# Fixed places for weight splits, and matmuls moved into the waits of two recurrences

## The chip, the cores and the metric

The program runs on one core of a Trainium2 chip. The metric is the device time in microseconds (us) of one execution. Five engines work side by side, each through its own list of instructions in order: TensorE (PE, matmuls and the weight loads before them), VectorE (DVE), ScalarE (ACT), GpSimd (POOL) and SyncE (SP, which only issues DMAs here). They wait for each other by semaphores.

## What is computed

One layer of a decoder for 512 prompt tokens and 8 samples of 4 tokens (544 columns in all): a SwiGLU feed-forward block, then time mixing (RWKV-7) beside a short gated convolution, then a second feed-forward block, with a layer norm after each. The part around the change is the time mixing. For each head of 64 the state S goes through all tokens:

```
S <- S diag(w) + (S (-kk)) (kk*a)^T + v k^T ;  o = S r
o = group_norm(o) ;  o = o + (sum r*k*r_k) v ;  y = o * g
mix = concat(y, y_conv) @ w_out
```

`g` is the gate, a low-rank product of its own (`sigmoid(gd) @ g_lora_up`), which does not depend on S. The prompt starts from S = 0, each sample from a stored S.

## The kernel before

All matrices lie transposed: features on the 128 partitions, tokens along the free dimension, in two halves (`HALF`: 256 and 288 columns). Matrix products of full precision are made of three matmuls: every weight tile is loaded in fp32 (`raw`), copied by ACT into a rounded high part (line 135 of `wsplit`), and DVE subtracts to get the low part (line 136). High times high, high times low and low times high add up in PSUM (`mm3`, lines 152 to 154). Such a tile of 1024 columns is called a weight, and its two operations a **split**. Two `raw` buffers and three or four split buffers (`hl`) turn over.

The 512 prompt tokens are cut into 8 chunks of 64. The heads go in two groups (g = 0, 1) of two tiles of two heads. For a group the kernel first builds the chunks' triangular matrices (`scores`, `elim`, `rounds`), and then goes through the chunks in order (`chain`, called from `recur`). This is the **recurrence**, and one chunk is a **step**, 0 to 7. A step is a chain over the engines: PE makes a product with the state (line 1230); ACT copies it to `W` (1233); PE multiplies by the inverse `XT` (1239); DVE copies one half of U (1240) and ACT the other (1241); PE multiplies by `BK` (1248); DVE adds this to S and scales it (1256, 1258), which makes the S of the next step. The output of the step before is made on the side (`out_u`, 1209; `out_s`, 1215; copy to `O` in 1217).

While the step's last DVE operations run, PE works on **fillers**: generators in the queue `bg` that yield their expected time; `slots` puts one step and then some 1500 ns of fillers in turn (18 matmuls). In the first recurrence the fillers are the convolution's products (`conv`, `conv_mm`: three weights for each of the tiles i = 0, 1, 2), in the second the output projection (`wout0`, then `wout1`, with weights `wo_c` and `wo_0`, and `last0` with `wo_1`). Inside a step PE has nothing else to do but small work that `small(c, k)` starts at three places of step c: k = 0 between 1230 and 1239, k = 1 between 1239 and 1248, k = 2 after the state update. That small work is

- `sample`: the samples' part of the recurrence. It loads the stored states (1285), makes two blocks of 32 small matmuls with them (1293), copies the results (1299 to 1303), makes a step like the prompt's (1308, 1315, 1324), and then for each of two tiles a product with its masked U (1333) and two DVE operations on the states (1335, 1336), and stores them (1338). The table `when` says at which (c, k) it goes on.
- `gnorm(g, 0, ...)`: the group norm of the first half of the columns: a product that centres (1349), a square (1350), the mean (1354), Ln and Exp (1355, 1357), the gate's product (1362), and three DVE operations with gain, bias and gate (1365 to 1367). Its first two parts run in step 5, the last after step 7. `gnorm(g, 1, ...)` does the second half after the recurrence.

PSUM has eight buffers: three named `mm` (from `big`), five named `sm` (from `sm`). Waits between engines and the buffers' turns are worked out when the program is built, from what reads and writes what. The order on each engine is worked out then too: a planner goes through expected durations and issues, on each engine, what is ready, the instruction traced first by the program going first. `after(x, y)` and `issue_after(y)` add an order (x not ahead of y on that engine) and no wait on the chip. In `slots`, what the fillers after step c trace may not stand ahead of the U copy and the state update of step c - 1. What is traced after the recurrence, outside of `slots`, has no such bound.

Of the kernel before, what the change touches and what calls it, by code (L numbers as in the profile page):

```python
# [14 lines left out]
AF = mybir.ActivationFunctionType  # L15
# [4 lines left out]
P = 128  # L20
# [41 lines left out]
def body(ctx: ExitStack, tc: tile.TileContext, xT, gu1, wd1, win, wo_c, wo_0, wo_1, gu2, wd2, wl, ln3, eye, lora, vec, cst,  # L62
# [30 lines left out]
    def sm():  # L93
        return ps.tile([P, 512], F32, name="sm", bufs=5)
# [39 lines left out]
    def wsplit(hl, raw, a, b):  # L134
        seen["hi"] = ACT.activation(hl[:, 0, a:b], raw[:, a:b], AF.Copy)  # L135
        seen["lo"] = DVE.tensor_tensor(hl[:, 1, a:b], raw[:, a:b], hl[:, 0, a:b].bitcast(F32), op=OP.subtract)  # L136
        return seen["lo"]

    def split(hi, lo, x):
# [16 lines left out]
                yield 6 * ((c1 - c0) / 2.4 + 3)  # L156

    bg = deque()
    seen = dict(rs=None, hhl=None, pe=None, fill=None, uv=None, new=[], old=[])

    def crit(e):
        seen["pe"] = e
# [1029 lines left out]
    def v2(q, rows=slice(0, P)):  # L1192
        return q[rows, :128].rearrange("p (d t) -> p d t", d=2)

    def chain(g, cp, small):


        tl = cp.tile
        AR = ARs[g]
        heads = [(pl, par) for pl in range(2) for par in range(2)]  # L1200
        Ss, q2, uv = {}, None, []

        def at(q, pl, par):
            return q[R(par), pl * 64:pl * 64 + 64]

        def out_u(c):
            q = sm()
            for pl, par in heads:
                crit(PE.matmul(at(q, pl, par), UV[:, pl, par, c, :], SC[:, pl, par, c, 64:128], start=(pl == 0 or c == 0),
                               stop=(c == 0), skip_group_check=True))  # L1210
            return q

        def out_s(c, q):
# [3 lines left out]
            o = ACT.activation(O[:, :, c, :], v2(q), AF.Copy)  # L1217
            for e in uv:
                after(o, e)

        for c in range(8):
            if c < 7:
                Sn = Ss[c + 1] = tl([P, 2, 2, 64], F32, name="S", bufs=3)
                with tc.issue_after(seen["pool"].ins):
                    for par in range(2):
                        POOL.tensor_copy(Sn[R(1 - par), :, par, :], UV[R(1 - par), :, par, c + 1, :])
            q = sm()
            for pl, par in heads:
                k = slice(0, P) if c else R(1 - par)
                crit(PE.matmul(at(q, pl, par), SC[k, pl, par, c, 0:64], Ss[c][:, pl, par, :] if c else UV[k, pl, par, c, :],  # L1230
                               start=True, stop=True))
            W = tl([P, 2, 64], F32, name="W", bufs=2)
            ACT.activation(W, v2(q), AF.Copy)
            if c:
                q2 = out_u(c - 1)
            small(c, 0)
            qs = (sm(), sm())
            for pl, par in heads:
                crit(PE.matmul(at(qs[par], pl, par), XT[R(par), c, pl, :], W[R(par), pl, :], start=True, stop=True))
            seen["uv"] = DVE.tensor_copy(UV[R(0), :, 0, c, :], v2(qs[0], R(0)))  # L1240
            seen["new"] = [ACT.copy(UV[R(1), :, 1, c, :], v2(qs[1], R(1)))]
            uv[:] = seen["new"]
            if c:
                out_s(c - 1, q2)
            small(c, 1)
            q = sm()
            for par, pl in heads:
                crit(PE.matmul(at(q, pl, par), BK[:, pl, par, c, :], UV[:, pl, par, c, :], start=True, stop=True))
            pe = Pe[:, 2 * g:2 * g + 2, c:c + 1].to_broadcast([P, 2, 64])
            if c == 7:  # L1250
                SF = tl([P, 2, 64], F32, name="W", bufs=2)
            for par in range(2):
                dst = Sn[R(par), :, par, :] if c < 7 else SF[R(par)]
                src = v2(q, R(par))
                if c:
                    DVE.tensor_tensor(dst, Ss[c][R(par), :, par, :], src, op=OP.add)
                    src = dst
                upd = DVE.tensor_tensor(dst, src, pe[R(par)], op=OP.mult)
            seen["new"].append(upd)
            small(c, 2)  # L1260
            if c == 7:
                dma(wkvp_o[:, 2 * g:2 * g + 2, :], SF)
                out_s(7, out_u(7))
            yield 1

    def recur(g, cp, run):
        sam, gn = sample(g, cp), gnorm(g, 0, cp)
        when = {(2, 0): 1, (2, 1): 1, (2, 2): 1, (3, 0): 1, (3, 1): 1, (4, 2): 1, (5, 2): 2, (6, 2): 2}

        def small(c, k):  # L1270
            for _ in range(when.get((c, k), 0)):
                next(sam, None)
            if c == 5 and k < 2:
                next(gn, None)

        slots(chain(g, cp, small), run)
        for x in (sam, gn):
            for _ in x:
                pass

    def sample(g, cp):
# [3 lines left out]
        dma(S0, s0[:, 2 * g:2 * g + 2])  # L1285
        WT = tl([P, 2, 32], F32, name="WT")
        SI = tl([P, 2, 2, 64], F32, name="SI")
        q = sm()
        qv = q[:, :256].rearrange("p (d x t) -> p d x t", d=2, x=2)
        for pl in range(2):  # L1290
            for b in range(NSEQ):
# [45 lines left out]
            yield 500  # L1337
        dma(wkvs_o[:, 2 * g:2 * g + 2], S0)

    def gnorm(g, h, cp):  # L1340
        t0, t1, _ = SEG[h]
        n = (256, 288)[h]
        t1 = t0 + n
# [10 lines left out]
            PE.matmul(q[:, :n], bo, sq[pl][:, :n], start=True, stop=True)  # L1354
            ACT.activation(sq[pl][:, :n], q[:, :n], AF.Ln, scale=1.0 / 64, bias=epsg)
        for pl in range(2):
            ACT.activation(sq[pl][:, :n], sq[pl][:, :n], AF.Exp, scale=-0.5)
        yield 600
        for pl in range(2):
            p = 2 * g + pl  # L1360
            qs.append(sm())
            PE.matmul(qs[pl][:, :n], lo[:, 1, P * p:P * p + P], sgd[:, t0:t1], start=True, stop=True)
        for pl in range(2):
            p, y = 2 * g + pl, sq[pl]
            DVE.scalar_tensor_tensor(y[:, :n], xc[pl][:, :n], col(V_GNG, p), sq[pl][:, :n], op0=OP.mult, op1=OP.mult)
            DVE.scalar_tensor_tensor(y[:, :n], y[:, :n], col(V_GNB, p), bvs[g][pl][:, t0:t1], op0=OP.add, op1=OP.add)
            DVE.tensor_tensor(o[pl], y[:, :n], qs[pl][:, :n], op=OP.mult)
            if g == 0:
                dma(ycd[:, p, t0:t1], o[pl])
            else:  # L1370
                split(xhl[:, 0, p, t0:t1], xhl[:, 1, p, t0:t1], o[pl])
# [18 lines left out]
    def conv(i):  # L1390
        u = tl([P, 2 + TP + 6 * NSEQ], F32, name="cu")
        cc = tl([P, T], F32, name="cc")
        zc = tl([P, T], F32, name="zc")
        us = u[:, 514:].rearrange("p (b t) -> p b t", t=6)
        POOL.memset(u[:, 0:2], 0.0)
        POOL.tensor_copy(us[:, :, 0:2], cst_[:, i])
        for h in range(2):
            yield from conv_mm(14 + 3 * i, h, partial(conv_c, cc))
        for h in range(2):
            yield from conv_mm(15 + 3 * i, h, partial(conv_u, cc, u, us))  # L1400
        taps = conv_taps(i, u, us, zc)
        next(taps)
        for h in range(2):
            for n, x in enumerate(conv_mm(16 + 3 * i, h, partial(conv_z, zc))):
                if n in (0, 2):
                    next(taps, None)
                yield x
            for _ in taps:
                pass
        dma(ycd[:, 4 + i], zc)  # L1410

    def conv_mm(i, h, use):
        c0, c1 = HALF[h]
        w = wget(i)
        q = big()
        yield from mm3(q[:, :c1 - c0], w, xhl, range(KD), c0, c1)
        use(q, h, c0, c1)
        yield 300
# [73 lines left out]
    cst0 = ExitStack()  # L1492
    cp = pool(cst0, "chain0")
    slots(rounds(0), 600)
    recur(0, cp, 1500)
    weave("g0", gnorm(0, 1, cp))
    cst0.close()
    ast.close()
    w4 = pool(ast, "w4")
    wstate["ex_hl"] = [lambda: w4.tile([P, 2, 1024], F32R, name="hl", bufs=1)]  # L1500
    weave("s2", pairs[2].scores())
    bg.appendleft(own_b(3))
    need(3, 2)
    take(FILL["p3"])
# [42 lines left out]
            for k, y in ys + [(7, zc)]:  # L1547
                ysplit(k, y, c0, c1)

    w1s, fin = {}, []  # L1550

    def add_z(d, h, o, n=1):
        c0, c1 = HALF[h]
# [3 lines left out]
    def wout0():  # L1557
# [41 lines left out]
    def wout1():  # L1599
# [66 lines left out]
    ast.close()  # L1666
    mst.close()
    yst.close()

    f2.s1[0] = s1  # L1670
    f2.open()
# [97 lines left out]
```

## Time and profile before

| | us |
|---|---|
| three timed runs | 1072.36, 1072.5, 1072.72 |
| median | 1072.5 |
| the profiled execution | 1072.43 |
| its span, first to last instruction | 1070.7 |
| PE busy | 1050.7 |
| DVE / ACT / POOL busy | 844.7 / 583.2 / 154.9 |
| first recurrence, steps 0 to 7 | from 503.9 to 544.1 |
| second recurrence, steps 0 to 7 | from 617.5 to 658.3 |

The recurrences' times are from PE's timeline: the first matmul of line 1230 in step 0, and the first filler after step 7's output. The mean clock granted to PE was 0.998 of full speed. A time like 504.76 is us from the span's start; "L1239" is line 1239 of the kernel before; "idle before" in brackets is how long an engine stood still ahead of an instruction, and which instruction of another engine ended that. A matmul's end is modelled and overlaps the next, so what an instruction costs PE is read from one start to the next.

### The profile page before, as it was taken

To read this page: it belongs to the slowest core of one execution; us is meant where nothing else is said; L and a number is where in the kernel's file an instruction comes from. 1 tells how busy PE (TensorE), PEld (TensorE's weight loads), DVE (VectorE), ACT (ScalarE), POOL (GpSimd) and SP (SyncE) were. 2 spreads that over 40 slices of the span, in tenths; PEclk is the share of its full clock that TensorE was granted. 3 is DMA by queue.
4 is the path that set the end of the run, shared out by engine and by line. 5 is a ranking of instruction groups with operands and counts; after the bars stand their busy time and mean duration, and the time that the engine had idled before them with its cause. 6 is when DMAs were issued, how large, how long until landed. Compare 5 with 4: busy or idle time off the path is not lost.

```text
span 1070.7 us, 22612 instructions
## 1 busy us (share of the span) xinstructions
PE 1050.7 (98%) x9178; PEld 1010.5 (94%) x9178; DVE 844.7 (79%) x1557; ACT 583.2 (54%) x1070; POOL 154.9 (14%) x273
## 2 busy tenths in 40 slices
PE   9999999999999999999999999999999999999997
PEld 8999999999999999899889988999999999999996
DVE  6797888979875777793578657988979888797757
ACT  5746555555553668654444435767555555555524
POOL 0111121211200022133101200001211212121000
PEclk9999999999999999999999999999999999999999
DMA  8558585676854233324145724434766848668512
GB/s 292 132 112 186 120 199 135 145 172 132 186 118 158 79 88 109 85 82 99 41 143 161 173 81 139 141 119 79 152 165 137 200 101 194 143 137 189 147 43 84
DMA packets 91528, 144.48 MB, mean 135 GB/s; under 512 B 34848, under 2 KB 52384, under 8 KB 91296
## 3 DMA queue, kind: packets, MB, share of 16 engines
q1 hardware_dynamic: 68144, 110.76, 34.2%
q0 software_dynamic: 22848, 31.72, 19.2%
q8 instruction: 72, 1.18, 0.4%
q10 hardware_dynamic: 432, 0.56, 0.2%
q14 instruction: 32, 0.26, 0.1%
HBM read 128.81 MB, written 9.75 MB: 129 GB/s over the span
## 4 chain that ended last, share of the span: by engine, by line
PE 76%; DVE 13%; ACT 7%; issue 2%; DMA 2%; POOL 0%; ACTq 0%; DVEq 0%; SPq 0%
PE mm L553 9%; PE mm L554 9%; PE mm L555 9%; PE sm L553 6%; PE sm L554 6%; PE sm L555 6%; PE mm L152 6%; PE mm L153 5%; PE mm L154 5%; DVE hhl L141 2%; ACT hl L135 2%; DVE hl L136 2%; PE sm L441 1%; PE sm L1166 1%; PE mm L784 1%
## 5 line engine op out<-in xcount | busy, mean ns | idle before, releaser
L136 DVE TENSOR_TENSOR hl<-raw,hl 128x1024 fp32r<-128x1024 f32 (+3 forms) x230 | 270.2, 1179 | 63.7 <-ACT hl L135 62.6
L135 ACT ACTIVATE hl<-raw 128x1024 fp32r<-128x1024 f32 (+3 forms) x230 | 232.9, 1020 | 69.7 <-DVE raw L519 43.5
L152 PE MATMUL mm<-xhl,hl 128*128 128x256 f32 (+1 forms) x704 | 209.2, 299 | 0.5 <-ACT xhl L140 0.5
L153 PE MATMUL mm<-xhl,hl 128*128 128x256 f32 (+1 forms) x704 | 203.0, 289 | 0.4 <-DVE xhl L141 0.4
L154 PE MATMUL mm<-xhl,hl 128*128 128x256 f32 (+1 forms) x704 | 202.0, 287 | 0.0
L152 PEld LDWEIGHTS mm<-xhl,hl 128*128 128x128 f32 x704 | 132.0, 188 | 6.9 <-issue 2.0
L153 PEld LDWEIGHTS mm<-xhl,hl 128*128 128x128 f32 x704 | 132.3, 188 | 2.7 <-issue 1.0
L154 PEld LDWEIGHTS mm<-xhl,hl 128*128 128x128 f32 x704 | 132.3, 188 | 0.3 <-issue 0.2
L555 PE MATMUL sm<-xhl,hl 128*128 128x272 f32 x432 | 125.2, 290 | 0.0
L554 PE MATMUL sm<-xhl,hl 128*128 128x272 f32 x432 | 124.4, 288 | 0.0
L553 PE MATMUL sm<-xhl,hl 128*128 128x272 f32 x432 | 124.1, 287 | 0.0
L553 PE MATMUL mm<-tv,hl 128*128 128x272 f32 x288 | 83.3, 289 | 0.3
L555 PE MATMUL mm<-tv,hl 128*128 128x272 f32 x288 | 83.4, 290 | 0.0
L554 PE MATMUL mm<-tv,hl 128*128 128x272 f32 x288 | 83.1, 288 | 0.0
L553 PEld LDWEIGHTS sm<-xhl,hl 128*128 128x128 f32 x432 | 81.4, 188 | 0.0
L554 PEld LDWEIGHTS sm<-xhl,hl 128*128 128x128 f32 x432 | 81.3, 188 | 0.0
L555 PEld LDWEIGHTS sm<-xhl,hl 128*128 128x128 f32 x432 | 81.2, 188 | 0.0
L532 POOL DMA_DIRECT2D raw<-in_wd x32 | 39.2, 1462 | 288.0 <-DVE hlb L141 225.2
L526 POOL DMA_DIRECT2D raw<-in_gu x36 | 43.3, 1203 | 203.5 <-DVE hlb L141 143.8
L553 PE MATMUL mm<-hhl,hl 128*128 128x272 f32 x192 | 56.4, 300 | 0.3
L554 PE MATMUL mm<-hhl,hl 128*128 128x272 f32 x192 | 55.9, 291 | 0.8 <-DVE hhl L141 0.2
L553 PEld LDWEIGHTS mm<-tv,hl 128*128 128x128 f32 x288 | 54.2, 188 | 1.9 <-ACT cpb L620 1.9
(416 smaller groups left out, 2716.0 us busy)
## 6 DMA issues: line engine op xcount, KB each, us to landing
raw<-in_gu SPq DMA_DIRECT2D x84, 512.0 KB, 4.5
raw<-in_gu POOLq DMA_DIRECT2D x36, 512.0 KB, 6.6
raw<-in_wd SPq DMA_DIRECT2D x32, 512.0 KB, 4.5
raw<-in_win SPq DMA_DIRECT2D x26, 512.0 KB, 3.6
raw<-in_wd POOLq DMA_DIRECT2D x32, 256.0 KB, 6.0
z<-sv POOLq DMA_DIRECT2D x16, 272.0 KB, 8.4
raw<-in_wo_c SPq DMA_DIRECT2D x8, 512.0 KB, 3.6
raw<-in_wd SPq DMA_DIRECT2D x8, 384.0 KB, 3.2
```

The source lines that it names most:

```text
L135: seen["hi"] = ACT.activation(hl[:, 0, a:b], raw[:, a:b], AF.Copy)
L136: seen["lo"] = DVE.tensor_tensor(hl[:, 1, a:b], raw[:, a:b], hl[:, 0, a:b].bitcast(F32), op=OP.subtract)
L141: return DVE.tensor_tensor(lo, x, hi.bitcast(F32), op=OP.subtract)
L152: PE.matmul(out, wh, src[:, 0, k, c0:c1], start=(start and i == 0), stop=False)
L153: PE.matmul(out, wh, src[:, 1, k, c0:c1], start=False, stop=False)
L154: seen["fill"] = PE.matmul(out, wl, src[:, 0, k, c0:c1], start=False, stop=(stop and i == n - 1))
L441: PE.matmul(o[i][h][:, :c1 - c0], block(hl, v, k), xhl[:, y, k, c0:c1], start=(k == 0 and j == 0), stop=(k == KD - 1 and j == 2), skip_gro ...
L526: POOL.dma_start(x.rearrange("p (s c) -> p s c", s=2), bass.AP(tensor=a11.tensor, offset=a11.offset, ap=[[2 * D, P], [P * 2 * D, 2], [1, 5 ...
L532: POOL.dma_start(four(x)[:, i], bass.AP(tensor=a11.tensor, offset=a11.offset, ap=[[DFF, P], [P * DFF, 2], [1, 256]]), accum_op=OP.add)
L553: PE.matmul(out, wh, src(0, i), start=(first and i == 0), stop=False, skip_group_check=True)
L554: PE.matmul(out, wh, src(1, i), start=False, stop=False, skip_group_check=True)
L555: PE.matmul(out, wl, src(0, i), start=False, stop=(i == n - 1), skip_group_check=True)
```

## The change

Four edits, which hang together.

1. **Places for splits.** While `seen["step"]` is set, a split's ACT operation is ordered after an ACT instruction and its DVE operation after a DVE instruction. Each step sets them to its own U copy and state update; `gnorm(0, 1)` sets them to its last Exp and last product; behind the scores of pair 2 and behind the second layer norm's first half it is cleared.
2. **Earlier tracing of loads.** `conv_mm` traces the load and split of the next weight at its own second half, one half ahead of use. `wout0` traces each weight one or two output tiles ahead, and the first two weights of `wout1` in its last two tiles.
3. **The samples' two blocks of products** go from (2, 0) and (2, 1) to (1, 1) and (2, 0), the copies after them from (2, 2) to (2, 1), and the last product with its DVE operations from (6, 2) to (7, 2). The accumulator of the blocks is an `mm` buffer and no longer an `sm`.
4. **The first half's gate products** are made in step 0, one at k = 0, one at k = 1; ACT copies both to SBUF after the U copy (into `pairs[3].sw` and `lnq`, which are free then). `gnorm(g, 0)` reads these copies in line 1367 and makes no product of its own.

```diff
     def wsplit(hl, raw, a, b):
         seen["hi"] = ACT.activation(hl[:, 0, a:b], raw[:, a:b], AF.Copy)
         seen["lo"] = DVE.tensor_tensor(hl[:, 1, a:b], raw[:, a:b], hl[:, 0, a:b].bitcast(F32), op=OP.subtract)
+        if seen["step"]:
+            after(seen["hi"], seen["step"][1])
+            after(seen["lo"], seen["step"][0])
...
             seen["new"].append(upd)
+            seen["step"] = upd, uv[0]
             small(c, 2)
...
-    def recur(g, cp, run):
-        sam, gn = sample(g, cp), gnorm(g, 0, cp)
-        when = {(2, 0): 1, (2, 1): 1, (2, 2): 1, (3, 0): 1, (3, 1): 1, (4, 2): 1, (5, 2): 2, (6, 2): 2}
+    def recur(g, cp, run, gt):
+        gs = []
+
+        def gates():
+            for pl in range(2):
+                p = 2 * g + pl
+                gs.append(sm())
+                PE.matmul(gs[pl][:, :256], lo[:, 1, P * p:P * p + P], sgd[:, 0:256], start=True, stop=True)
+                if pl:
+                    for x, q in zip(gt, gs):
+                        after(ACT.activation(x, q[:, :256], AF.Copy), uv[0])
+                yield 0
+
+        ga = gates()
+        sam, gn = sample(g, cp), gnorm(g, 0, cp, gt)
+        when = {(1, 1): 1, (2, 0): 1, (2, 1): 1, (3, 0): 1, (3, 1): 1, (4, 2): 1, (5, 2): 2, (7, 2): 2}
...
+            if c == 0 and k < 2:
+                next(ga)
...
-        q = sm()
+        q = big()
         qv = q[:, :256].rearrange("p (d x t) -> p d x t", d=2, x=2)
...
+            if gt:
+                qs.append(gt[pl])
+                continue
             qs.append(sm())
             PE.matmul(qs[pl][:, :n], lo[:, 1, P * p:P * p + P], sgd[:, t0:t1], start=True, stop=True)
...
-            DVE.tensor_tensor(o[pl], y[:, :n], qs[pl][:, :n], op=OP.mult)
+            m = DVE.tensor_tensor(o[pl], y[:, :n], qs[pl][:, :n], op=OP.mult)
+            if h and not g:
+                seen["step"] = m, e
...
-    def conv_mm(i, h, use):
+    def conv_mm(i, h, use, nxt=0):
         c0, c1 = HALF[h]
         w = wget(i)
+        if h and nxt:
+            wget(nxt)
...
-    recur(0, cp, 1500)
+    recur(0, cp, 1500, [pairs[3].sw[:, 256 * pl:256 * pl + 256] for pl in range(2)])
...
     weave("s2", pairs[2].scores())
+    seen["step"] = None
...
         for d in range(KD):
+            if d % 2 == 0 and d:
+                wc = wn
             if d == 4:
-                w0 = wload(wo_0[1])
+                w0 = w0n
+            if d == 2:
+                w0n = wload(wo_0[1])
+            if d in (1, 3, 5):
+                wn = wload(wo_c[d // 2 + 1])
+            if d == 6:
+                pre.append(wload(wo_c[0]))
+            if d == 7:
+                pre.append(wload(wo_0[0]))
             if d > 1:
-                if d % 2 == 0:
-                    wc = wload(wo_c[d // 2])
...
-            if d % 2 == 0:
+            if d == 0:
+                wc, w0 = pre
+            elif d % 2 == 0:
                 wc = wload(wo_c[d // 2])
-            if d == 0:
-                w0 = wload(wo_0[0])
...
-    recur(1, cp, 1500)
+    recur(1, cp, 1500, [lnq[:, pl, 0:256] for pl in range(2)])
...
+    seen["step"] = None
```

More of the change, by code (lines that the diff above doesn't have):

```diff
@@ L158, in body @@
     bg = deque()
-    seen = dict(rs=None, hhl=None, pe=None, fill=None, uv=None, new=[], old=[])
+    seen = dict(step=None, rs=None, hhl=None, pe=None, fill=None, uv=None, new=[], old=[])
     def crit(e):
@@ L1193, in v2 @@
         return q[rows, :128].rearrange("p (d t) -> p d t", d=2)
+    uv = []
     def chain(g, cp, small):
@@ L1200, in chain @@
         heads = [(pl, par) for pl in range(2) for par in range(2)]
-        Ss, q2, uv = {}, None, []
+        Ss, q2 = {}, None
+        uv[:] = []
         def at(q, pl, par):
@@ L1338, in sample, with gnorm @@
         dma(wkvs_o[:, 2 * g:2 * g + 2], S0)
-    def gnorm(g, h, cp):
+    def gnorm(g, h, cp, gt=None):
         t0, t1, _ = SEG[h]
@@ L1356, in gnorm @@
         for pl in range(2):
-            ACT.activation(sq[pl][:, :n], sq[pl][:, :n], AF.Exp, scale=-0.5)
+            e = ACT.activation(sq[pl][:, :n], sq[pl][:, :n], AF.Exp, scale=-0.5)
         yield 600
@@ L1396, in conv @@
         POOL.tensor_copy(us[:, :, 0:2], cst_[:, i])
+        j = 14 + 3 * i
         for h in range(2):
-            yield from conv_mm(14 + 3 * i, h, partial(conv_c, cc))
+            yield from conv_mm(j, h, partial(conv_c, cc), j + 1)
         for h in range(2):
-            yield from conv_mm(15 + 3 * i, h, partial(conv_u, cc, u, us))
+            yield from conv_mm(j + 1, h, partial(conv_u, cc, u, us), j + 2)
         taps = conv_taps(i, u, us, zc)
@@ L1403, in conv @@
         for h in range(2):
-            for n, x in enumerate(conv_mm(16 + 3 * i, h, partial(conv_z, zc))):
+            for n, x in enumerate(conv_mm(j + 2, h, partial(conv_z, zc), j + 3 if i < 2 else 0)):
                 if n in (0, 2):
@@ L1548, in conv_last @@
                 ysplit(k, y, c0, c1)
-    w1s, fin = {}, []
+    w1s, fin, pre = {}, [], []
     def add_z(d, h, o, n=1):
```

## The prediction, made before the result was known

> **What bounds the kernel now.** I read the page first: how long, and which engine is full.
>
> ```profile
> span 1070.7 us, 22612 instructions
> PE 1050.7 (98%) x9178; PEld 1010.5 (94%) x9178; DVE 844.7 (79%) x1557; ACT 583.2 (54%) x1070; POOL 154.9 (14%) x273
> PE 76%; DVE 13%; ACT 7%; issue 2%; DMA 2%; POOL 0%; ACTq 0%; DVEq 0%; SPq 0%
> ```
>
> TensorE (PE) is busy for 98% of the span and carries 76% of the chain that ended last. Its order is fixed by the program, so a microsecond in which it waits is a microsecond of the end, and little else is: the whole program leaves it 1070.7 - 1050.7 = 20.0 us of idle time. The other engines matter only where PE stands still for them. So the second view is who PE waited for, in the two stretches that hold the recurrences (498 to 600 us, 600 to 700 us). Columns: engine, tile and line, whom it waited for, us in total, times, longest.
>
> ```profile
> PE sm L1248 <- DVE UV L1240: 1.7, 4, 0.7
> PE sm L1057 <- DVE gq L1365: 0.6, 1, 0.6
> ...
> PE sm L1248 <- DVE UV L1240: 1.7, 4, 0.6
> PE sm L1248 <- ACT O L1217: 0.3, 1, 0.3
> ```
>
> In each recurrence PE stops four times, 1.7 us in all, ahead of the products that use U (L1248); once it stops 0.6 us for a buffer that the group norm holds (L1365), once 0.3 us for one that the output copy holds (L1217). These rows hold 4.3 us, four tenths of a per cent; the prize is little more. The third view is PE's timeline, step by step.
>
> **The gate products in step 0.** Columns: start, us, engine, line, operation, tiles, count, and in brackets the idle time before.
>
> ```profile
> 503.93 0.45 PE L1230 MATMUL sm<-UV,SC 64*64 64x64 f32 x8
> 504.76 0.45 PE L1239 MATMUL sm<-W,XT 64*64 64x64 f32 x8 [0.38 <-ACT W L1233]
> 505.57 0.46 PE L1248 MATMUL sm<-UV,BK 128*64 128x64 f32 x8 [0.37 <-DVE UV L1240]
> ...
> 546.40 1.02 PE L1362 MATMUL sm<-cpb 128*128 128x256 f32 x4
> 547.26 1.13 PE L1349 MATMUL sm<-O,cs 128*128 128x288 f32 x4
> ...
> 513.63 1.10 PE L1293 MATMUL sm<-AR,DM 64*64 64x8 f32 x32
> 514.59 0.43 PE L1239 MATMUL sm<-W,XT 64*64 64x64 f32 x8
> ```
>
> Today's gate products (L1362, two of two instructions) take PE from 546.40 to 547.26: 0.86 us, or 0.43 for each. The change makes one between L1230 and L1239 of step 0, the other between L1239 and L1248, where PE idles 0.38 and 0.37 us. Does it fit? Small matmuls issue 32 in 0.96 us (513.63 to 514.59), so a group of eight takes about 0.24; 0.24 + 0.43 = 0.67 against the 0.83 (503.93 to 504.76) and 0.81 (504.76 to 505.57) that the steps take anyway. So they cost nothing there, and 0.86 disappears later. The dearer row for a pair among small matmuls is 0.62 (next fence, 656.68 to 657.30 is where the held matmuls resume; I read it as an upper bound since a wait lies in it); then 0.24 + 0.62 = 0.86 and each gap would overrun by 0.05. Gain 0.70 to 0.86; I take **0.80**.
>
> In the second recurrence L1362 stands elsewhere:
>
> ```profile
> 656.18 0.45 PE L1248 MATMUL sm<-UV,BK 128*64 128x64 f32 x4
> 656.68 0.70 PE L1362 MATMUL sm<-cpb 128*128 128x256 f32 x2
> 657.30 0.39 PE L1248 MATMUL sm<-UV,BK 128*64 128x64 f32 x3
> 658.29 0.40 PE L152 MATMUL mm<-xhl,hl 128*128 128x288 f32 x1
> 660.77 0.59 PE L1362 MATMUL sm<-cpb 128*128 128x256 f32 x2
> ...
> 543.11 0.46 PE L1248 MATMUL sm<-UV,BK 128*64 128x64 f32 x8 [0.71 <-DVE UV L1240]
> 544.11 0.40 PE L152 MATMUL mm<-xhl,hl 128*128 128x288 f32 x1
> ...
> 655.54 1.06 ACT L135 ACTIVATE hl<-raw 128x1024 fp32r<-128x1024 f32 x1 [0.22 <-DMA raw<-in_wo]
> ```
>
> Here step 7 falls apart: only four of the eight L1248 run at 656.18; the others need the half of U that ACT copies, and ACT is inside a weight split until 656.60 (655.54 + 1.06). From the first L1248 to the next filler takes 2.11 us, against 1.00 for the same step of the first recurrence (543.11 to 544.11). With the gates gone and the split pinned behind the copy, 1.11 goes, and the second pair's 0.43: 1.54. If the split stays in front, only the two pairs go, 0.86. I take **1.50**.
>
> The four copies that bring the gates to SBUF are new work on ACT. In step 0 ACT is idle:
>
> ```profile
> 507.69 0.38 ACT L1421 ACTIVATE cc<-mm 128x256 f32<-128x256 f32 x1 [2.15 <-PE mm L154]
> ```
>
> This row is such a copy (128x256 out of PSUM): 0.38, and 2.15 us of idle time before it take two, 0.76. Without that cover the next step's copy of W would be late by 0.76 at most, per recurrence. [...] I go by the row's idle time: the copies hide, and what they buy is the PSUM buffer, which would otherwise be held for seven steps.
>
> **The samples' products in step 1.**
>
> ```profile
> 509.23 0.45 PE L1239 MATMUL sm<-W,XT 64*64 64x64 f32 x8 [0.17 <-ACT W L1233]
> 510.04 0.46 PE L1248 MATMUL sm<-UV,BK 128*64 128x64 f32 x8 [0.37 <-DVE UV L1240]
> ...
> 516.07 0.46 PE L1248 MATMUL sm<-UV,BK 128*64 128x64 f32 x8
> ...
> 536.24 0.45 PE L1239 MATMUL sm<-W,XT 64*64 64x64 f32 x8
> 537.05 0.46 PE L1248 MATMUL sm<-UV,BK 128*64 128x64 f32 x8
> ...
> L1299 DVE COPY SC<-sm x2: 217/217/217, 516.2 to 629.3; 64x64 f32<-64x64 f32 x2
> L1285 SPq DMA_DIRECT2D DM<-in_s x2: 327/330/333, 502.9 to 616.5; - x2
> DMA to landing us min/median/max: 3.7/4.4/5.1
> ```
>
> Step 1 takes 0.81 from L1239 to L1248 today and will take 0.24 + 0.96 = 1.20 with 32 L1293 inside: +0.39. Step 2 takes 1.48 (514.59 to 516.07) and falls to the bare latency of 0.81 (536.24 to 537.05): -0.67. Net -0.28. The copies of the products' results (L1299, 0.22) now come up just where step 2 copies U; the planned order may put one in front. So -0.28 to -0.06; I take 0.15 for each recurrence, **0.30**. The states that the products read must have landed: issued at 502.9 plus 5.1 at most is 508.0, before 509.5; in the second recurrence 616.5 + 5.1 = 621.6, before 622.9. The products' accumulator moves to a "mm" buffer: one filler group has two instead of three for one slot, which holds less than two groups. The POOL fills that follow the copies move up by one phase with them and are used in step 3 as before. The last state product (L1333) and its two DVE operations go from step 6 to step 7: PE pays the same there, and the store of the samples' state moves back on SP's queue, behind one weight load.
>
> **Splits with a place.** A pin is an order on ACT and DVE, no wait on a semaphore: queued behind a pinned split stands whatever comes later in that engine's order.
>
> ```profile
> 541.71 0.45 PE L1239 MATMUL sm<-W,XT 64*64 64x64 f32 x8
> ...
> 541.64 1.22 DVE L136 TENSOR_TENSOR hl<-raw,hl 128x1024 fp32r<-128x1024 f32 x1
> 542.78 0.27 DVE L1240 COPY UV<-sm 64x128 f32<-64x128 f32 x1
> ...
> 551.69 1.06 ACT L135 ACTIVATE hl<-raw 128x1024 fp32r<-128x1024 f32 x1 [0.70 <-DMA raw<-in_win]
> 552.78 1.23 DVE L136 TENSOR_TENSOR hl<-raw,hl 128x1024 fp32r<-128x1024 f32 x1 [0.52 <-ACT hl L135]
> 553.92 0.51 DVE L1365 SCALAR_TENSOR_TENSOR gq<-sm,vc,gq 128x288 f32<-128x288 f32 x1
> ```
>
> Step 7 of the first recurrence: DVE starts a split at 541.64 and copies U only at 542.78, so L1239 to L1248 is 1.40 (541.71 to 543.11) where step 6 needs 0.81. This split belongs to a load that the program traces after the recurrence; pinned, it cannot stand there, and the move of two sample operations out of step 6 empties DVE further. Gain 0 to 0.59; I take **0.59**. Behind the group norm a split on both engines (551.69, 552.78) pushes L1365 to 553.92, and PE's 0.6 us wait is for that buffer. The load traced in this place is now pinned behind the norm; another, traced later, stays free and could take the gap. Gain 0 to 0.64; I take **0.64**: in this row no other work stands in front of L1365.
>
> The other pins change little: loads are now traced one half earlier and pinned one step later than the old rule, which comes to the same step in most cases. So steps 4 to 6 keep their waits. One pin costs: the first weights of wo_1.
>
> ```profile
> 656.84 1.21 DVE L136 TENSOR_TENSOR hl<-raw,hl 128x1024 fp32r<-128x1024 f32 x1
> ...
> 661.96 0.50 PE L152 MATMUL mm<-xhl,hl 128*128 128x256 f32 x1
> ...
> L1335 DVE TENSOR_TENSOR DM<-DM,sm 128x512 f32<-128x512 f32 x4 | 2.8, 688 | 0.1
> ```
>
> Today its low half is ready at 658.05, 3.9 us before the first matmul that can use it (661.96). Pinned, it comes after step 7's state update, and the samples' two operations (2 x 0.69) now stand there too. Between nothing and one whole split, 1.21; I take **+0.30**, since 3.9 us of slack cover most.
>
> **Sum.** -0.80 - 1.50 - 0.30 - 0.59 - 0.64 + 0.30 = -3.53. The profiled execution took 1072.43 (span 1070.7 and 1.7 around it), the median of the runs shown is 1072.5, 0.07 more. Forecast **1068.9**. About 0.2%, 2.1 us, is what a measurement of this kernel can tell from no change, so "faster" means below 1070.4.
>
> **The rivals.**
> - *More than forecast.* The waits left in steps 4 to 6 are 1.7 + 1.7 + 0.3 less the four 0.37 and the 0.71: about 1.5; if a third of that stays, 1.0 goes. For it: less is queued on DVE. Against: the same splits in the same steps. 1067.9.
> - *A buffer too few.* Step 0 now allocates six "sm" tiles of five. The 0.3 us wait on L1217 is such a wait. At 0.25 in four places, 1.0: 1069.9. [...] Against: the first of the six is free once W is copied, long before the sixth.
> - *The change doesn't do what it says:* a pin is only a lower bound; free loads slip into the places left. Then 0.59, 0.64 and 0.70 of the 1.50 stay: -3.53 + 1.93 = -1.60, 1070.8, no measurable change.
> - *wo_1 late.* Both its loads late by a whole split, 2 x 1.21 less the 0.30 counted: 1071.0.
> - *Slower: weights late inside the recurrences.* Eight loads are split there. A pinned split needs 1.06 + 1.22 = 2.28 us after its step's copy and update; where it ends behind the first filler matmul that reads it, PE stands still, up to 2.28 each. Three of the eight cost 6.8: 1075.7. It decides as soon as two are late by a whole split more than was won. For it: the pins forbid splitting ahead. Against: each load is traced a half (24 matmuls) ahead, and PE shows no wait for weights there today.
>
> **Chances.** Forecast 0.46, more 0.10, buffer 0.06: faster 0.62. Slipped splits 0.18, wo_1 0.08: same 0.26. Late weights 0.12: slower. The range leaves out late weights and the ends of the rest: 1067.0 (the better case, with all 1.5 of its waits gone, and the gates and products at their best: 1067.9 - 0.5 - 0.1 - 0.3) to 1072.0 (wo_1 late, the products and both gate terms at their worst: 1071.0 + 0.2 + 0.1 + 0.6 = 1071.9).
>
> **What would show it.** In step 0, L1362 between the three groups with no idle time in brackets, and none after step 7. L1293 in steps 1 and 2. No split between L1239 and its copies of U in step 7 of either recurrence, and L1057 without its wait. The four rows of PE's waits down from 4.3 us to under 2. A row of PE L152 waiting for DVE hl or ACT hl in either stretch would prove me wrong, as would a long wait before the first wo_1 matmul.

## The result and the profile after

The changed kernel took **1079.26 us** (median of 12 runs, 1075.51 to 1083.56) against 1072.69 for the kernel before beside it: a ratio of 1.0056, 95% interval 1.0042 to 1.0070. By the ratio it is slower by 6.0 us, where 1068.9 was forecast, outside the range (1067.0 to 1072.0).

The runs spread by 8 us, and the spread follows the granted clock of PE that is listed with each run: four at 0.999 took 1075.5 to 1076.2, eight at 0.990 to 0.996 took 1077.9 to 1083.6. The change so costs about 3 us at full clock, and in two of three runs PE loses clock as well. The profiled execution is of the second kind (1077.85 us, clock 0.996). Line numbers of the changed kernel are higher by 3 in the helpers and by some 6 to 30 below; each is named as it comes up.

The page of the changed kernel, the lines that answer to those of before:

```profile
span 1076.1 us, 22607 instructions
PE 1055.4 (98%) x9178; PEld 1013.0 (94%) x9178; DVE 844.7 (79%) x1557; ACT 583.7 (54%) x1074; POOL 159.4 (15%) x273
PE 77%; DVE 13%; ACT 6%; issue 2%; DMA 1%; POOL 0%; ACTq 0%; DVEq 0%; SPq 0%
```

PE is still the bound. It made the same 9178 matmuls, yet is busy 4.7 us longer (1055.4 against 1050.7), while its idle time hardly moved (20.7 against 20.0). The same work and more busy time stand here beside a lower mean clock, 0.996 against 0.998. Then PE's waits, from 498 to 604 us (the four rows ahead of the dots) and from 604 to 706 us: us in total, times, longest.

```profile
PE sm L1074 <- DVE SC L1063: 1.3, 2, 1.0
PE sm L1093 <- DVE SC L1063: 1.2, 1, 1.2
PE sm L1060 <- DVE bkb L1040: 0.5, 1, 0.5
PE sm L1254 <- DVE UV L1246: 0.2, 1, 0.2
...
PE mm L157 <- DVE hl L136: 1.3, 1, 1.3
PE sm L1254 <- DVE UV L1246: 1.0, 2, 0.6
PE mm L155 <- DVE z L1586: 0.8, 1, 0.8
PE sm L1254 <- ACT O L1223: 0.3, 1, 0.3
```

Line 1254 is the old 1248: its waits for U fell from 3.4 to 1.2 us, and the wait for the group norm's buffer (L1057 <- L1365) is gone. In their place stand new ones, none of them a term of the prediction's sum: for the score masks of pairs 2 and 3 (L1063, before 1060) and for an operand of pair 3's scores (`bkb`, L1040), *behind* the first recurrence; for the low half of a weight (L136) in step 0 of the second, which only a rival had priced; and for the sums of the output projection (L1586) behind it. They come to 5.1 us; before, the scores of pair 3 held 0.6.

The windows of 5 us behind the first recurrence (length, then busy us of PE, PEld, DVE, ACT, POOL, then PEclk, the granted clock; the last two columns are DMA), and a narrower one:

```profile
555.00:560.00 5.00, 3.79 (x38) 2.72 (x36) 3.09 (x7) 0.87 (x3) 0.00 (x0) 0.80 0.83 251
560.00:565.00 5.00, 5.00 (x26) 4.14 (x27) 1.39 (x3) 4.46 (x11) 0.00 (x0) 0.52 0.01 1
565.00:570.00 5.00, 5.00 (x42) 5.00 (x42) 4.94 (x9) 0.75 (x2) 1.17 (x2) 1.00 0.38 101
...
558.00:561.00 3.00, 3.00 (x32) 2.15 (x31) 0.09 (x1) 1.20 (x5) 0.00 (x0) 0.50 0.65 191
```

The narrow row shows the clock at one half. At half clock for 5 x 0.20 / 0.5 = 2.0 us of the first row and 5 x 0.48 / 0.5 = 4.8 of the second, PE ran 6.8 us at half speed, which cost it 3.4, from 558.0 on, 1.6 us behind the end of the 1.2 us wait (556.35). In stretches of 0.5 us the clock reads 1.00 up to 558.0, 0.50 up to 564.5, 0.67 in the next and 1.00 from 565.0 on, so it is taken as either half or full in such sums. The kernel before shows 1.00 in all three rows; its middle one:

```profile
560.00:565.00 5.00, 5.00 (x46) 4.63 (x42) 4.34 (x7) 3.17 (x10) 0.00 (x0) 1.00 0.12 25
```

### The profile page after: what moved, and what is told of

Its sections match the earlier page's. It is cut to its first block, busy times and chain, and to the rows that moved or that the text cites. A ratio compares the mean times of both kernels' runs of the same rounds, so it can differ in the third digit from the quotient of the medians.

```text
span 1076.1 us, 22607 instructions
## 1 busy us (share of the span) xinstructions
PE 1055.4 (98%) x9178; PEld 1013.0 (94%) x9178; DVE 844.7 (79%) x1557; ACT 583.7 (54%) x1074; POOL 159.4 (15%) x273
## 4 chain that ended last, share of the span: by engine, by line
PE 77%; DVE 13%; ACT 6%; issue 2%; DMA 1%; POOL 0%; ACTq 0%; DVEq 0%; SPq 0%
PE mm L556 9%; PE mm L557 9%; PE mm L558 9%; PE mm L155 6%; PE sm L556 6%; PE sm L557 6%; PE sm L558 6%; PE mm L156 6%; PE mm L157 6%; DVE hhl L144 2%; DVE hl L136 2%; PE sm L444 1%; ACT hl L135 1%; PE sm L1169 1%; PE mm L787 1%
## 5 line engine op out<-in xcount | busy, mean ns | idle before, releaser
L136 DVE TENSOR_TENSOR hl<-raw,hl 128x1024 fp32r<-128x1024 f32 (+3 forms) x230 | 270.2, 1179 | 59.1 <-ACT hl L135 58.0
L155 PE MATMUL mm<-xhl,hl 128*128 128x256 f32 (+1 forms) x704 | 209.9, 299 | 1.5 <-DVE z L1586 0.8
L155 PEld LDWEIGHTS mm<-xhl,hl 128*128 128x128 f32 x704 | 132.5, 189 | 7.6 <-issue 1.9
```

Source lines behind the costliest of these rows:

```text
L155: PE.matmul(out, wh, src[:, 0, k, c0:c1], start=(start and i == 0), stop=False)
```

## The experiments

Three theories. **A**: the fixed places themselves cost; splits kept out of one stage come up in the next, on DVE ahead of what PE waits for. **B**: the moved gates and samples cost. **C**: the clock falls behind a wait of PE, as it did 1.6 us behind the one of 1.2 us (PE busy for 3.79 of the 5 us from 555 on), so a wait among small matmuls costs more than its length. Each kernel below was timed beside the kernel before (medians 1072.67 to 1072.97).

### One part alone, and all but the places

`a1_gates`: only the gate products in step 0.

```diff
+            if c == 0 and k < 2:
+                next(ga)
```

> The kernel before with the gate products alone moved to step 0 of each recurrence (their copies to SBUF as in the changed kernel; no places for splits, loads and samples as before). Theory A (splits held back by their fixed places pile up on DVE after the first recurrence and in step 0 of the second): this part is free of it. The trace of the changed kernel shows the pair of products costing 0.37 us more in each step 0 and 0.86 less later, so 0.5 gained per recurrence at most: 1071.5 to 1072.7. Theory B (the moved gates themselves cost: products among small matmuls and copies on ACT ahead of the splits): 1074 to 1076, and PE waits for a weight's half in step 0 of the second recurrence here too. Theory C (the clock: a wait in the scores of pair 2 lets the granted clock fall): no wait there, so the clock stays at 0.998 or more in every run.

Measured: 1072.52, ratio 0.9999 (0.9990 to 1.0007). The moved gates are worth nothing, and cost nothing. In the trace each step 0 grows by 0.37 us, and PE waits behind each recurrence (498 to 604 us, then 604 to 720):

```profile
PE sm L1057 <- DVE O L1388: 1.2, 1, 1.2
...
PE sm L226 <- ACT hhl L140: 1.0, 1, 1.0
```

What the removed pair frees is taken back there: 1.2 us for the group norm's buffer, where it was 0.6, and 1.0 us in a layer norm (L226), which has no row in the same view of the kernel before.

`a2_samples`: only the new `when` and the `mm` accumulator.

```diff
-        when = {(2, 0): 1, (2, 1): 1, (2, 2): 1, (3, 0): 1, (3, 1): 1, (4, 2): 1, (5, 2): 2, (6, 2): 2}
+        when = {(1, 1): 1, (2, 0): 1, (2, 1): 1, (3, 0): 1, (3, 1): 1, (4, 2): 1, (5, 2): 2, (7, 2): 2}
```

> The kernel before with the samples' products alone moved (first in step 1, last state product in step 7, accumulator in the larger kind of buffer). Theory A: not touched by it; the changed kernel's step 1 is 0.2 us longer and its step 2 0.69 shorter than before, so 0.2 to 0.5 gained per recurrence: 1071.6 to 1072.7. Theory B': the moved samples cost, since step 7 now carries the last state product and its two DVE operations: 1073.5 or more. Theory C: clock unchanged, no spread between the runs.

Measured: 1070.43, ratio 0.9978 (0.9969 to 0.9987): a gain of 2.3 us, more than any theory had. PE's timeline, steps 6 and 7 of the first recurrence, in the kernel before and in this one:

```profile
535.41 0.45 PE L1230 MATMUL sm<-S,SC 128*64 128x64 f32 x8
...
540.88 0.45 PE L1230 MATMUL sm<-S,SC 128*64 128x64 f32 x8
```

```profile
535.15 0.45 PE L1230 MATMUL sm<-S,SC 128*64 128x64 f32 x8
...
539.77 0.45 PE L1230 MATMUL sm<-S,SC 128*64 128x64 f32 x8
...
541.77 0.46 PE L1248 MATMUL sm<-UV,BK 128*64 128x64 f32 x8 [0.49 <-DVE UV L1240]
542.16 1.13 PE L1333 MATMUL sm<-ux,BS 128*128 128x512 f32 x2
...
543.98 0.41 PE L152 MATMUL mm<-xhl,hl 128*128 128x288 f32 x1
```

Step 6 takes 4.62 us (535.15 to 539.77); before it took 5.47 (535.41 to 540.88). The two products of line 1333 stood there on top of the step's fillers; now they follow step 7's L1248. Step 7 gives that back: from its start to its first filler it takes 4.21 us (539.77 to 543.98), before 3.23 (540.88 to 544.11). The gain lies elsewhere. Steps 1 and 2 together are 0.49 shorter in the first recurrence and 0.44 in the second. PE's 0.6 us wait for the norm's buffer is gone, without any place: DVE now has both L1365 ahead of the split (before, the split stood first: 552.78, then 553.92):

```profile
551.52 0.52 DVE L1365 SCALAR_TENSOR_TENSOR gq<-sm,vc,gq 128x288 f32<-128x288 f32 x1
...
552.75 1.22 DVE L136 TENSOR_TENSOR hl<-raw,hl 128x1024 fp32r<-128x1024 f32 x1
```

And step 7 of the second recurrence no longer falls apart: all eight L1248 run at 654.10. So step 6 wins 0.84 there, and step 7 grows by only 0.10 (3.85 against 3.75), with the two L1333 in it and a pair of gate products out of it.

`a3_pins_loads`: places and earlier loads alone. `a4_no_pins`: the changed kernel without the places.

```diff
-        if seen["step"]:
+        if False:
```

> The kernel before with the places of the splits and the earlier loads alone; gates and samples as before. Theory A: most of the loss is here. At full clock PE stops 1.2 us in the scores of pair 2, 1.0 to 1.8 in those of pair 3, 1 or more for a weight in the second recurrence, 0.8 in the first norm behind it, less 0.6 won in step 7: 1074 to 1077 in the fastest runs. Theory B (gates and samples): 1071 to 1072.5. Theory C: if PE stops over 1 us in the scores of pair 2, some runs show a granted clock of 0.990 to 0.996 and are 3 to 7 us longer than the fastest; if it doesn't stop, none does.

> The changed kernel without the places of the splits: earlier loads, gates and samples stay. Theory A: the places are the cause, so the loss goes, and what gates and samples win is left: 1070.0 to 1072.5, every run at a clock of 0.998 or more. If the earlier loads alone are enough to pile splits up in the wrong place, 1073 to 1076. Theory B: stays at 1075 or more at full clock. Theory C: the clock falls only where PE stops over 1 us in the scores.

Measured: a3 1078.28 (1075.74 to 1081.51), ratio 1.0041 (1.0027 to 1.0054); a4 1070.05 (1069.51 to 1070.33), ratio 0.9973 (0.9961 to 0.9984), all its runs at 0.998 or more. B falls: with the places the kernel is slower, without them faster than before.

### Which place

`b1_pins_first`: places in the first recurrence and behind the norm only. `b2_pins_second`: in the second only. `b3_steps_only`: in both, but dropped when the first recurrence is traced, and none behind the norm. The edits of b1 and b3 (b2 has `if g:`):

```diff
-            seen["step"] = upd, uv[0]
+            if not g:
+                seen["step"] = upd, uv[0]
```

```diff
-            if h and not g:
-                seen["step"] = m, e
...
     recur(0, cp, 1500, ...)
+    seen["step"] = None
```

> The changed kernel with fixed places only in the first recurrence and the group norm behind it; in the second recurrence splits are free. The kernel without any places took 1070.05, the changed one 1075.6 in its fastest runs and 1079.3 in the median. Theory A1 (the loss at full clock is in the second recurrence: a weight late in step 0 and DVE full in the norm behind it): the fastest runs are at 1070 to 1071.5; PE still stops about 1.2 us in the scores of pair 2, and by theory C (clock) some runs lose 3.4 us or a multiple of it at a granted clock of 0.996 or less, so the median is 1072 to 1075. Theory A2 (the loss is behind the first recurrence): the fastest runs are at 1073 to 1076.

> The changed kernel with fixed places only in the second recurrence. Theory A1: the fastest runs are at 1072.5 to 1074.5, with PE stopped 1.3 us for the low half of a weight in step 0 of the second recurrence; no stop of 1.2 us in the scores of pair 2 and none of 1.0 in those of pair 3. Theory A2: 1070 to 1071. Theory C: the clock can fall only behind the 1.3 us stop in the second recurrence, so fewer runs lose it than in the changed kernel.

> The changed kernel with the places dropped as soon as the first recurrence is traced: splits traced behind it aren't held behind the group norm. Splits traced inside the recurrences keep their places. Theory D (the norm's place pushes two splits in front of the score masks): no stop of 1.2 us in the scores of pair 2, no loss of clock there, and the fastest runs as in the kernel with places only in the second recurrence, about 1072.5 to 1074.5. Theory E (splits held back inside the steps are late anyway, wherever the last place is): the stop stays and the fastest runs are at 1075 or more.

Measured: b1 1075.79 (1074.01 to 1077.56), every run at a clock of 0.992 to 0.996; b2 1073.10 (1072.23 to 1074.78); b3 1073.44 (1072.48 to 1074.70), the latter two at 0.997 or more. Against a4 (1070.05) the first recurrence with its norm costs 5.7 us, the second 3.1; together 8.8 of the 9.2 that lie between a4 and the changed kernel. So neither A1 nor A2, as b1 and b2 set them against each other, holds alone: b1's fastest run, 1074.0, lies where A2 put it, b2's, 1072.2, close to where A1 did, and the places cost in both stretches. Theory D holds: without the norm's place the long score waits are gone (the longest there is 0.3 us in b3) and no run lies below a clock of 0.997, and the second recurrence's waits are left (b3, 604 to 720 us):

```profile
PE mm L157 <- DVE hl L136: 1.3, 1, 1.3
...
PE mm L155 <- DVE z L1585: 0.9, 1, 0.9
```

`c1_first_steps`: places inside the first recurrence alone (both edits above). `c4_first_steps_no_gates`: the same, with the gates where they were.

> The changed kernel with fixed places only for splits traced inside the first recurrence: none behind the group norm, none in the second recurrence. Theory A1 (places in the second recurrence cost 3 to 4 us, the norm's place costs the stops in the scores and the clock; places inside the first recurrence gain): the trace of the kernel with places in both recurrences but not behind the norm reaches the second elimination 1.05 us ahead of the kernel without places, so 1070.05 - 1.05 = 1069.0, range 1068.5 to 1069.8, clock 0.998 or more. Theory E (held-back splits cost wherever they are): 1070.5 or more.

> As the kernel with places inside the first recurrence alone, but with the gate products where they were before. Alone the moved gates changed nothing (1072.52 against 1072.69), with a stop of 1.0 us in the first norm behind the second recurrence taking back what they had won there. Theory G (with the earlier loads that stop doesn't come, so the gates are worth their 0.5 us per recurrence): 1069.5 to 1070.5, slower than with the gates by 0.5 to 1. Rival (the gates are worth nothing): within 0.4 us of the kernel with the gates.

Measured: c1 **1069.77** (1068.74 to 1070.24), ratio 0.9968 (0.9957 to 0.9980), faster than both kernels; c4 1070.21, ratio 0.9974 (0.9965 to 0.9983). Theory E falls. b1 and c1 differ only in what holds the splits that are traced behind the first recurrence (step 7's place until the norm sets its own, then the norm's; called the place behind the norm from here on), and that is 6.0 us, as A1 of c1 has it. In the profiled executions (1073.4 against 1068.4 us of span) the waits behind the recurrence are 2.7 us longer in b1 (3.9 against 1.2), and 3.4 us more at half clock are another 1.7; about 0.6 is not told apart. c1 against a4 (0.3) and c1 against c4 (0.4) lie within their intervals: the gain that A1 expected of the places inside the first recurrence is not shown, and theory G and its rival are not decided.

How one place does that is read from DVE's timeline, the changed kernel first, then c1:

```profile
549.37 0.52 DVE L1390 SCALAR_TENSOR_TENSOR gq<-sm,vc,gq 128x288 f32<-128x288 f32 x1 [4.13 <-ACT gq L1379]
...
552.15 1.22 DVE L136 TENSOR_TENSOR hl<-raw,hl 128x1024 fp32r<-128x1024 f32 x1
553.28 1.28 DVE L1063 TENSOR_TENSOR SC<-sm,cs 128x512 f32<-128x512 f32 x2
554.48 1.22 DVE L136 TENSOR_TENSOR hl<-raw,hl 128x1024 fp32r<-128x1024 f32 x1
555.61 1.48 DVE L1063 TENSOR_TENSOR SC<-sm,cs 128x512 f32<-128x512 f32 x3
```

```profile
546.04 1.22 DVE L136 TENSOR_TENSOR hl<-raw,hl 128x1024 fp32r<-128x1024 f32 x1 [0.64 <-ACT hl L135]
549.53 0.52 DVE L1391 SCALAR_TENSOR_TENSOR gq<-sm,vc,gq 128x288 f32<-128x288 f32 x1 [2.27 <-ACT gq L1380]
...
552.17 1.23 DVE L136 TENSOR_TENSOR hl<-raw,hl 128x1024 fp32r<-128x1024 f32 x1 [0.34 <-ACT hl L135]
553.31 0.45 DVE L1393 TENSOR_TENSOR O<-gq,sm 128x288 f32<-128x288 f32 x1
553.68 2.68 DVE L1063 TENSOR_TENSOR SC<-sm,cs 128x512 f32<-128x512 f32 x5
```

In c1 a split runs at 546.04, while DVE has nothing else; in the changed kernel it must wait for the norm's last Exp and product, DVE stands idle 4.13 us, and two splits come up later, one ahead of the masks and one among them. The five masks out of `sm` buffers take 2.68 us in one stretch in c1; with the split between them they take 3.81 (553.28 to 557.09). In pair 3 a split stands ahead of the masks again (at 575.39 in the changed kernel); that the two `raw` buffers pass the delay on from split to split is argued, not shown.

### The weight in step 0, and the earlier loads

`c2_not_step0`: b3 with places in the second recurrence from step 1 on. `c5_late_loads`: the changed kernel with the loads of before.

```diff
-            seen["step"] = upd, uv[0]
+            if not g or c:
+                seen["step"] = upd, uv[0]
```

> As the kernel with places inside both recurrences and not behind the norm (1073.44), but in the second recurrence places begin with step 1. Theory F (the 1.3 us stop in step 0 is one split pinned behind step 0's state update that is read at once): the stop goes and 1.3 to 1.7 us with it: 1071.7 to 1072.2; the 0.9 us stop in the first norm behind the recurrence stays. Rival (DVE and ACT are too full in step 0 to split in time, place or not): the stop stays and it takes 1073 or more.

> The changed kernel with the loads of before (each weight fetched when its first group of products is traced), all places kept. Theory H (a place needs an earlier load, and the changed kernel's loads are early enough in most places): more stops for weights in both recurrences, each up to 2.3 us: 1078 to 1090 in the fastest runs. Rival (earlier loads make no difference to a split with a fixed place, as the prediction had it for most of them): 1075 to 1077 in the fastest runs, stops as in the changed kernel.

Measured: c2 1071.42 (1069.87 to 1072.92), ratio 0.9988 (0.9979 to 0.9997), 2.0 us below b3, somewhat more than theory F's 1.3 to 1.7; the wait for L136 is gone, that for L1586 stays, and F holds. The changed kernel's timelines of ACT, DVE and PE show it:

```profile
623.12 0.39 ACT L1283 ACTIVATE lnq<-sm 128x256 f32<-128x256 f32 x1
623.40 1.05 ACT L135 ACTIVATE hl<-raw 128x1024 fp32r<-128x1024 f32 x1
...
625.06 2.35 DVE L136 TENSOR_TENSOR hl<-raw,hl 128x1024 fp32r<-128x1024 f32 x2
...
624.73 0.28 PE L156 MATMUL mm<-xhl,hl 128*128 128x256 f32 x1
626.33 0.38 PE L157 MATMUL mm<-xhl,hl 128*128 128x256 f32 x1 [1.33 <-DVE hl L136]
```

Held behind step 0's U copy, and behind a gate's copy of 0.39, ACT makes the high part at 623.40; DVE has the low part at about 626.2, and PE wanted it at 625.0. In c2 and before no split lies in step 0: these weights had been split ahead of the recurrence (the last at 614.59 in c2), which is just what a place forbids.

c5 took 1089.54 (1088.62 to 1090.55), ratio 1.0154 (1.0140 to 1.0168). Its waits from 604 to 706 us:

```profile
PE mm L157 <- DVE hl L136: 6.5, 4, 1.8
PE mm L155 <- ACT hl L135: 2.0, 2, 1.1
```

Theory H holds: the earlier loads save 10 us of what the places would cost, clock included; they only don't save all.

### The clock

`b4_masks_twice`: the kernel before, with the four large score masks of pair 2 computed twice.

```diff
                 for par, q in enumerate(qs):
-                    DVE.tensor_tensor(SC[:, pl, par, a0c:a0c + n, :], ...
+                    for _ in range(2 if p == 2 and n > 1 else 1):
+                        DVE.tensor_tensor(SC[:, pl, par, a0c:a0c + n, :], ...
```

> The kernel before with the four large score masks of pair 2 computed twice into the same place, nothing else: DVE needs 4 x 0.6 = 2.4 us more ahead of the transposes and PE has to wait for it. [...]

Measured: 1076.89 (1075.23 to 1081.97), ratio 1.0037 (1.0024 to 1.0050). Four runs at 0.998 or more took 1075.2 to 1076.2, five at 0.990 to 0.997 took 1076.9 to 1082.0. Its windows, then two of c1:

```profile
555.00:560.00 5.00, 4.64 (x42) 3.63 (x39) 5.00 (x11) 0.00 (x0) 0.00 (x0) 1.00 0.44 134
560.00:565.00 5.00, 5.00 (x43) 3.64 (x43) 1.42 (x4) 3.02 (x11) 0.00 (x0) 0.80 0.26 56
565.00:570.00 5.00, 5.00 (x22) 4.52 (x21) 4.30 (x8) 1.25 (x2) 0.00 (x0) 0.52 0.00 0
```

```profile
570.00:575.00 5.00, 4.22 (x46) 3.42 (x43) 3.64 (x7) 1.63 (x4) 0.29 (x2) 0.88 0.50 137
575.00:580.00 5.00, 5.00 (x45) 4.14 (x45) 2.21 (x4) 1.95 (x8) 0.00 (x0) 0.78 0.66 124
```

Without a single place the clock falls in the same stage, again for 2.0 + 4.8 = 6.8 us: the fall came without the places. But the stop that was expected did not come: PE's longest wait in that stage is 0.9 us, since the planned order spread fillers between the score products instead. So the clock fell here with no wait of 1 us. In c1 the stage of pair 3 lost 5 x 0.12 / 0.5 + 5 x 0.22 / 0.5 = 3.4 us at half clock, half of the other two, and PE waited at no time between 550 us and that fall (573.7) for longer than 0.37 us. Nor did it fall in the score stages alone: in c5 the clock falls in the recurrences, near waits of 0.8 to 1.8 us for weights, first in the first one:

```profile
517.50:524.00 6.50, 5.70 (x42) 5.12 (x42) 1.28 (x2) 0.28 (x1) 0.00 (x0) 0.50 0.27 81
```

It does so three times in the second one, from about 640.2, 653.8 and 667.4 us, in all 6.8 + 3.4 + 3.4 + 6.8 = 20.4 us at half clock against 6.8 in the changed kernel (mean clock 0.988 against 0.996). That is an estimated 6.8 us of the 12.7 by which the profiled execution of c5 is longer (1090.55 against 1077.85). The kernel before is not free of it either: 18 of its 71 runs beside the experiments show a clock of 0.996 or 0.997 and took 1073.4 to 1074.2. What makes the clock fall stays open. PE's busy time does not tell the kernels apart: in the 5 us from 570 on it is 4.22 us in c1, whose clock falls there, and 4.22 and 4.21 in b2 and b3, whose clock reads 1.00 in every window from 545 to 590. The second recurrence's 1.3 us wait, amid full-size matmuls, cost no clock in the profiles of b2 and b3 either (1.00 in each window from 620 to 635).

## Why the prediction was wrong, step by step

- **Gates, "they cost nothing there".** Wrong in size. PE's timeline of the changed kernel, step 0 of the first recurrence and, behind the dots, its step 7 (for a later point):

```profile
503.84 0.45 PE L1236 MATMUL sm<-UV,SC 64*64 64x64 f32 x8
504.22 0.70 PE L1280 MATMUL sm<-cpb 128*128 128x256 f32 x2
504.85 0.45 PE L1245 MATMUL sm<-W,XT 64*64 64x64 f32 x8
505.23 0.70 PE L1280 MATMUL sm<-cpb 128*128 128x256 f32 x2
505.86 0.46 PE L1254 MATMUL sm<-UV,BK 128*64 128x64 f32 x8
...
540.66 0.45 PE L1245 MATMUL sm<-W,XT 64*64 64x64 f32 x8
...
541.48 0.46 PE L1254 MATMUL sm<-UV,BK 128*64 128x64 f32 x8
```

  A pair takes 0.63 (504.22 to 504.85), close to the 0.62 that the prediction had named as its upper bound, and the group ahead of it 0.38, where 0.24 was taken. 1.01 per gap does not fit into 0.83 and 0.81: each step 0 lost 0.38. The gain behind was there, but a1 shows that the next wait takes it. Forecast -0.80 and the gates' part of -1.50; measured 0.
- **Samples, -0.30.** Steps 1 and 2 gave more than was priced: 0.20 to 0.26 lost and 0.69 won per recurrence, where 0.39 and 0.67 were worked out and 0.15 net was taken; 8 of the 32 products run ahead of L1245. "PE pays the same there" for the last state product holds in the first recurrence (0.85 won, 0.98 given back). But the move does in a2, without any place, what the sum had booked under the pins: it ends the wait for the norm's buffer (-0.64) and puts step 7 of the second recurrence together again (the split's part of -1.50). Measured -2.3, two thirds of the whole forecast.
- **The split's part of -1.50.** In the changed kernel all eight L1254 of that step 7 run at 660.77, as forecast; but so they do in a2 (654.10) and a4 (655.02), which have no places, and not in a1 (four at 656.90). It is the moved samples that do it.
- **Split in step 7, -0.59.** Came true: L1245 to L1254 takes 0.82 there (fence above, 540.66 to 541.48), where it took 1.40. The place behind the norm does it; in c1, without that place, a split stands ahead of U again and it takes 1.19 (540.46 to 541.65):

```profile
541.65 0.46 PE L1254 MATMUL sm<-UV,BK 128*64 128x64 f32 x8 [0.51 <-DVE UV L1246]
```

  The buffer's wait, -0.64: gone in the changed kernel, and the trace reaches pair 2's scores 1.25 us earlier than before (551.22 against 552.47). The place helps, for a4 and c1 wait 0.9 and 0.4 there; a2 shows that it is not the only way.
- **wo_1, +0.30.** No wait for its weights. The places did cost on that path, by another way: L155 waits 0.8 us for a PSUM buffer until DVE has made a sum (L1586). The changed kernel, b3 and c2 have this wait, a4 and c1 don't, so it comes with the places of the second recurrence; that splits ahead of the sum on DVE make it late is argued, for the norm's six operations stand there too.
- **"The other pins change little", and the norm's pin as a gain.** This step failed, and with it the sign. It asked whether a split would land in the same *step*, and never what comes behind the last one. The prediction counted what the pins behind the first recurrence win (0.59 + 0.64) and put at nothing what the held-back splits then delay: the next work on DVE, the masks. That place cost 6.0 us net, with its clock (b1 against c1). The places in the second recurrence were put at +0.30 and cost about 3 (b2 against a4), of which 2.0 lie in step 0 (c2 against b3).
- **The rivals.** "Weights late inside the recurrences" had 0.12 and 1075.7. Its mechanism is real (c5), but in the changed kernel one weight of eight was late, by 1.33 us. The row that was to prove the forecast wrong, PE waiting for DVE hl, did come. The clock was in no rival. Another sign came as foretold while the time went up: the four rows of waits are down from 4.3 to 1.5 us, but the cost stands behind the first recurrence, in rows that this sign did not cover.

Without the harmful places c1 reaches 1069.8, within 1 us of the forecast. That is luck: its terms are others than those of the sum.

Open: about 1 us of the second recurrence's 3 is in no wait that the trace names (b3 and a4 differ by 1.68 in step 0 and by some 2 from step 7 to the end, of which 0.9 is the wait for L1586). Open too: how the delay reaches pair 3, and what makes the clock fall.

## What to carry to other kernels

An order that keeps work out of a critical stretch only moves it; follow it to the first thing that PE waits for on that engine, and leave it free to run *ahead*, where the engine is idle. Drop such an order where its reason ends: here it did no measurable harm inside the first recurrence and cost 6 us one stage later. Where a large change moves little, try its parts alone: 2.3 us lay in one table and one buffer.

## What the hardware showed that was not expected

In the profiled execution of the changed kernel the granted clock fell to half for 6.8 us, without PE standing still for more than 1.33 us anywhere between 498 and 706 us; in other kernels it fell for 3.4 us (c1) or 6.8 us (b4) at a time. The mean clock says that it falls in eight of the twelve runs, by different amounts (0.990 to 0.996, against 0.999 in the other four). It differs from run to run of the same kernel, so such a kernel becomes not only slower but uneven: 8 us from the fastest run to the slowest, against 1.8 to 2.9 for the kernel before. The clock fell with no wait longer than 1.2 us in the stage ahead of it in the changed kernel, 0.9 in b4 and 0.4 in c1.
